# A two-layer hybrid decoder: who forms the low parts of the weights, and in what pieces

## The chip, the cores and the metric

The kernel runs on one core of a Trainium2 chip. The metric is the time of one execution on the device, in microseconds (us). The engines of a core go by short names here: PE is TensorE (matrix products; PEld is its loading of the stationary operand), DVE is VectorE, ACT is ScalarE, POOL is GpSimd, and SP is SyncE, which issues the transfers (DMA). Each engine works through its own queue in order.

## The reference

Two layers over 256 tokens of width 2048. Each layer is one mixer that adds to the residual stream; what matters here are its three products with large weights.

```python
for l in range(DEPTH):                      # DEPTH = 2
    shift, scale, gate = jnp.split(c_act @ w_ada[l] + b_ada[l], 3, axis=-1)
    h = rms_norm(x, norm_w[l]) * (1.0 + scale[:, None, :]) + shift[:, None, :]
    (gq, gk, gv, glr, gz, dq, dk, dv, da, db, dz, aq, ak, av, az) = jnp.split(h @ w_in[l], bounds, axis=-1)
    # o_gla: gated linear attention; o_gdn: gated delta rule; o_diff: differential softmax attention
    ...
    y = jnp.concatenate([o_gla, o_gdn, o_diff], axis=-1) @ w_out[l]
    x = x + gate[:, None, :] * y
```

All is float32: x is (1, 256, 2048), w_ada[l] 2048 x 6144, w_in[l] 2048 x 7704, w_out[l] 2048 x 2048.

## The kernel before

The program is written out in full (no loops on the device) and the order of each engine's instructions is chosen by a scheduler at build time, which goes by priorities: the weights' splitting and the modulation have priority AHEAD (1500), the mixers' steps 100000.

The modulation (w_ada) is one row vector times a matrix, so it is done on DVE: for each of the 24 groups of the two layers, eight transfers of 128 x 1024 land in a raw buffer, and DVE multiplies each by the vector and sums it along the row in one instruction (line 338, "rawa"). Layer 0's modulation and part of layer 1's run beside layer 0's input projection, and the rest beside what follows.

The input and output projections run on PE. To keep float32's precision with the faster float32r products, each factor is split into a high and a low part, and three products are summed: high by high, high by low, low by high. The activations' parts are hh and hl (lines 397 to 404; hn is the value before the split). The weights' parts are wh and wl. The function weights (line 303) does it: SP loads a chunk of up to 1024 columns into one of six raw buffers, which the modulation uses too (line 308, "raw"); the chunk is taken in pieces of at most 536 columns; ACT casts each piece to float32r (line 316, wh), and the difference to the raw piece is the low part (line 319, wl). A count decides the engine that subtracts: of each seven pieces in a row, three are given to POOL and four to DVE. There are five buffers each for wh and wl, of 536 columns.

project (line 433) uses a chunk in two ways. In the T form (tokens by columns) 512 columns of weights are the moving operand of two token tiles: six products per 512 columns, into the banks "pt". In the F form the weights are stationary, 128 columns at a time, into "pf". After the last k tile, or after each step's share of k tiles, the sums are added to what is there by DVE (line 450). out_project (line 1054) uses the weights as stationary operand, into "py", and DVE adds the gated sum to the residual (line 1200, xr). Between pieces poll() resumes the mixers, which are generators; they use all engines, and POOL does part of their elementwise work. Where the mixers take the mean square of heads, ACT writes the squares, which nobody reads, to a small tile, "junk".

Of the kernel before, what the change touches and what calls it, by code (L numbers as in the profile page):

```python
# [10 lines left out]
F32 = mybir.dt.float32  # L11
# [7 lines left out]
P = 128  # L19
D = 2048  # L20
KT = 16
T = 256
# [8 lines left out]
# The times (us) that the mixers' steps yield.  # L31
YW = {0: 7.0, 1: 8.0, 2: 25.0, 3: 1.25, 4: 2.0, 5: 2.0, 6: 15.0, 7: 2.5, 8: 11.25, 9: 3.25, 10: 6.0, 11: 4.0, 12: 2.94, 13: 0.75, 14: 1.5, 15: 3.0, 16: 3.0, 17: 3.5, 18: 2.0, 19: 3.75, 20: 6.25, 21: 7.5, 22: 3.75, 23: 10.0, 24: 14.0, 25: 0.75, 26: 3.75, 27: 7.0, 28: 2.25, 29: 12.0, 30: 4.2}

# Offsets of the input projection's columns, as the reference orders them.
# [19 lines left out]
# Blocks of columns in the order in which they are computed.  # L54
# [11 lines left out]
# The steps of each layer's input projection: blocks b0..b1-1 over k tiles k0..k1-1. (Layer 0's modulation arrives k tile  # L66
# by k tile, and layer 1's follows the norm.)
# [4 lines left out]
# The k tiles of the output projection's steps: gated linear attention, delta rule, differential attention.  # L72
# [3 lines left out]
def in_chunks(layer, i):  # L76
    """Chunks of w_in for one step: lists of (block, k0, k1) that share one transfer."""
# [23 lines left out]
def _chunk_pieces(chunk):  # L101
    """Sizes of the pieces, of whole k tiles, in which a chunk is split into two parts."""
    out = [0]
    for b, a, z in chunk:
        for _ in range(a, z):
            if out[-1] + _width(b) > 536:
                out.append(0)
            out[-1] += _width(b)
    return out


# Column layout of the packed per-partition parameters.
# [17 lines left out]
def _constants():  # L130
# [6 lines left out]
    # Of each chunk of 64 tokens, its own columns alone.  # L137
# [14 lines left out]
def hybrid_trunk(ctx: ExitStack, tc: tile.TileContext, x, cvec, pos, par, w_ada, w_in, w_out, w_lr, qkn, adt, cst, out):  # L152
# [7 lines left out]
    wsp = ctx.enter_context(tc.tile_pool(name="wsp", bufs=5))  # L160
# [8 lines left out]
    def reg(i, name):  # L169
        """One of the work tiles that the mixers hand on to each other, in the order of the program."""  # L170
        return work.tile([P, 512], F32, name=name, tag=f"R{i}", bufs=1)
# [4 lines left out]
    def bank(name, tag):  # L176
        """A PSUM bank. Each tag's banks are handed on in the order of the program: "a" delta rule and norm, "b" the other
        mixers, "p" projections."""
        return psum.tile([P, 512], F32, name=name, tag=tag, bufs=BANKS[tag])
# [4 lines left out]
    # The mixers are generators, resumed between pieces of the projections; they yield the tensor engine's time after which  # L184
    # their next step's inputs are expected, or a condition. PSUM banks and work tiles are handed on in this order.
# [46 lines left out]
    class Bank:  # L232
        """A PSUM bank (or half of its partitions) whose sums all rest on one clearing, by the first product. The products
        have to be issued in_order()."""
# [44 lines left out]
    junk = const.tile([P, 512], mybir.dt.bfloat16, name="junk")  # L279
# [21 lines left out]
    state = {"n": 0}  # L301

    def weights(src, sizes):
        """Loads sum(sizes) columns of weights and returns the two parts of each piece of them."""
        n = sum(sizes)
        raw = wraw.tile([P, RAW], F32, name="raw", tag="raw")
        with tc.high_priority(offset=AHEAD if state["n"] else 0):
            SP.dma_start(raw[:, 0:n], src)
        out, off = [], 0
        for m in sizes:  # L310
            r = raw[:, off:off + m]
            off += m
            wh = wsp.tile([P, 536], F32R, name="wh", tag="wh")[:, 0:m]
            wl = wsp.tile([P, 536], F32R, name="wl", tag="wl")[:, 0:m]
            with tc.high_priority(offset=AHEAD):
                ACT.copy(wh, r)  # L316
                state["n"] += 1
                e = POOL if state["n"] % POOL_WL[1] < POOL_WL[0] else DVE
                e.tensor_tensor(wl, r, wh.bitcast(F32), ALU.subtract)  # L319
            out.append((wh, wl))  # L320
        return out

# [1 line left out]
    ada = [const.tile([P, 3, KT], F32, name=f"ada{l}") for l in range(L)]  # L324

    def ada_group(l, g, raws=None):
        """Groups 0..7: scale and shift of k tiles 2g, 2g+1; groups 8..11: gate of k tiles 4(g-8)..+3."""
# [39 lines left out]
    def ada_mark(l, g):  # L367
        """Steps until the modulation's group g of layer l is done."""
        return 8 * (12 * l + g + 1)

# [4 lines left out]
    def rstd_rows(sqs):  # L375
        """sqs: tiles of squares whose sum over tiles and partitions is each token's. Returns its rstd on all partitions."""
# [20 lines left out]
    def modulate(l, xt, rb, hh, hl, k):  # L397
        """Two k tiles of the modulated input, in two parts."""
# [34 lines left out]
    def project(l, group, hh, hl, o, after):  # L433
# [18 lines left out]
        for chunk in in_chunks(l, group):  # L452
# [3 lines left out]
            parts = weights(src, _chunk_pieces(chunk))  # L456
            off = 0
            for b, a, z in chunk:
                kind = BLOCKS[b][0]
                w = _width(b)  # L460
                for k in range(a, z):
                    if off == parts[0][0].shape[1]:
                        parts.pop(0)
                        off = 0
                        poll()
                    wh, wl = parts[0]
# [624 lines left out]
    for l in range(L):  # L1091
# [132 lines left out]
        if l == 0:  # L1224
            sq = [temp("sqs", T, 1)]
# [81 lines left out]
```

## Time and profile before

| | |
|---|---|
| Median of 3 runs | 1144.73 us (1144.65 to 1145.38) |
| The profiled execution: span, first to last instruction | 1140.7 us |
| The profiled execution: whole time | not recorded apart; the median above lies 4.0 us over the span |
| PE busy | 1060.2 us (93%) |
| PEld busy | 927.9 us (81%) |
| DVE busy | 913.4 us (80%) |
| ACT busy | 613.7 us (54%) |
| POOL busy | 619.9 us (54%) |
| Read from memory | 267.76 MB, 238 GB/s over the span |

PE's products are pipelined and the ends of their records are modelled, so busy time of PE is not time at its peak. In stretches, the three projections and the mixers lie about so: layer 0's input projection from 27 to some 480 us, its output projection to 600 us, layer 1's input projection to some 1030 us, its output projection to the end.

### The profile page before, as it was taken

The numbers are of one execution on the slowest core, as the hardware profiler recorded it, in microseconds if no ns is written. First come the engines' busy times: TensorE is split into PE (matmuls) and PEld (weight loads), VectorE is DVE, ScalarE is ACT, GpSimd is POOL, SyncE is SP. The second block draws the span as 40 slices with busy tenths as digits, with TensorE's granted clock in tenths as the row PEclk, the third lists the DMA queues.
The fourth block names the chain that finished last, engine by engine and source line by source line (L and its number), as shares of the span: only waits on it lengthen the run. The fifth ranks groups of instructions, "written<-read, shape, count | busy, mean of one in ns | idle before, by whom it ended". The sixth has DMA issues, their size and how long they took to land.

```text
span 1140.7 us, 20595 instructions
## 1 busy us (share of the span) xinstructions
PE 1060.2 (93%) x7398; PEld 927.9 (81%) x7398; DVE 913.4 (80%) x1484; ACT 613.7 (54%) x1367; POOL 619.9 (54%) x550
## 2 busy tenths in 40 slices
PE   4989998889799999999988999998899999999998
PEld 3769876678788886898986877888799877879998
DVE  6899999998999759799788796767656877767853
ACT  4645434445654474666535545476454556557642
POOL 5444444456474586666753554366443666644642
PEclk9999999999999998999998999999899999999999
DMA  9888988888777454666689889785435555667462
GB/s 356 300 291 315 332 292 305 273 290 286 266 258 256 150 166 166 238 206 194 197 283 341 326 313 326 251 310 185 149 99 178 190 183 185 224 219 252 138 201 95
DMA packets 76807, 273.31 MB, mean 240 GB/s; under 512 B 8816, under 2 KB 9888, under 8 KB 76576
## 3 DMA queue, kind: packets, MB, share of 16 engines
q1 hardware_dynamic: 76704, 271.99, 69.8%
q8 instruction: 58, 0.95, 0.3%
q14 instruction: 45, 0.37, 0.1%
HBM read 267.76 MB, written 4.19 MB: 238 GB/s over the span
## 4 chain that ended last, share of the span: by engine, by line
PE 45%; DVE 25%; DMA 11%; issue 9%; POOL 5%; ACT 3%; SPq 0%; DVEq 0%; ACTq 0%; POOLq 0%
PE pt L191 21%; PE py L191 9%; DVE rawa L338 7%; DVE wl L319 7%; DMA rawa<-in_w_ada 7%; PE pf L191 6%; DMA raw<-in_w_in 4%; POOL wl L319 3%; DVE on_gdn L673 2%; PE Z_ps L191 1%; ACT wh L316 1%; PE o_gdn L191 1%; DVE z L450 1%; PE o_gla L191 1%; DVE hn L402 1%
## 5 line engine op out<-in xcount | busy, mean ns | idle before, releaser
L319 POOL TENSOR_TENSOR wl<-raw,wh 128x512 fp32r<-128x512 f32 (+2 forms) x266 | 403.8, 1532 | 355.8 <-ACT wh L316 319.1
L316 ACT CAST wh<-raw 128x512 fp32r<-128x512 f32 (+2 forms) x620 | 367.3, 613 | 311.2 <-PE pt L191 122.6
L338 DVE SCALAR_TENSOR_TENSOR rawa<-rawa,c_row 128x1024 f32<-128x1024 f32 x184 | 262.5, 1431 | 84.3 <-DMA rawa<-in_w_ada 73.0
L319 DVE TENSOR_TENSOR wl<-raw,wh 128x512 fp32r<-128x512 f32 (+2 forms) x354 | 285.5, 821 | 52.1 <-ACT wh L316 50.9
L191 PE MATMUL pt<-wl,hh 128*128 128x512 f32 (+1 forms) x768 | 294.1, 385 | 16.7 <-DVE wl L319 12.7
L191 PE MATMUL pt<-wh,hl 128*128 128x512 f32 (+1 forms) x768 | 289.2, 381 | 1.0 <-DVE hl L404 0.9
L191 PE MATMUL pt<-wh,hh 128*128 128x512 f32 (+1 forms) x768 | 257.4, 383 | 8.5 <-ACT hh L403 6.9
L191 PEld LDWEIGHTS pt<-wl,hh 128*128 128x128 f32 x768 | 146.3, 191 | 52.8 <-DVE wl L319 20.0
L191 PEld LDWEIGHTS pt<-wh,hh 128*128 128x128 f32 x768 | 144.5, 190 | 41.2 <-ACT hh L403 9.1
L191 PEld LDWEIGHTS pt<-wh,hl 128*128 128x128 f32 x768 | 145.8, 190 | 29.6 <-DVE hl L404 2.5
L191 PE MATMUL pf<-hh,wl 128*128 128x256 f32 x512 | 148.8, 292 | 6.4 <-POOL wl L319 4.0
L191 PE MATMUL pf<-hh,wh 128*128 128x256 f32 x512 | 148.2, 290 | 0.0
L191 PE MATMUL pf<-hl,wh 128*128 128x256 f32 x512 | 147.6, 289 | 0.0
L191 PEld LDWEIGHTS pf<-hh,wl 128*128 128x128 f32 x512 | 99.0, 194 | 9.5 <-POOL wl L319 4.9
L191 PEld LDWEIGHTS pf<-hh,wh 128*128 128x128 f32 x512 | 99.4, 194 | 2.3 <-issue 1.2
L191 PEld LDWEIGHTS pf<-hl,wh 128*128 128x128 f32 x512 | 99.1, 194 | 1.1 <-issue 0.7
L191 PE MATMUL py<-ogg,wh 128*128 128x256 f32 x512 | 99.4, 289 | 0.0
L191 PE MATMUL py<-odf,wh 128*128 128x256 f32 x512 | 91.6, 281 | 0.8 <-ACT odf L1044 0.7
L191 PEld LDWEIGHTS py<-ogg,wh 128*128 128x128 f32 x512 | 80.5, 189 | 0.9 <-issue 0.2
L191 PEld LDWEIGHTS py<-odf,wh 128*128 128x128 f32 x512 | 78.4, 188 | 1.5 <-ACT odf L1044 0.9
L191 PE MATMUL py<-odf,wl 128*128 128x256 f32 x256 | 72.0, 282 | 2.6 <-POOL wl L319 1.3
L191 PE MATMUL py<-ogg,wl 128*128 128x256 f32 x256 | 73.1, 287 | 0.0
(279 smaller groups left out, 1416.7 us busy)
## 6 DMA issues: line engine op xcount, KB each, us to landing
raw<-in_w_in SPq DMA_DIRECT2D x224, 512.0 KB, 4.6
rawa<-in_w_ada SPq DMA_DIRECT2D x184, 512.0 KB, 4.7
raw<-in_w_out SPq DMA_DIRECT2D x64, 512.0 KB, 4.2
raw<-in_w_in SPq DMA_DIRECT2D x20, 402.0 KB, 4.1
fr<-in_w_ada SPq DMA_DIRECT2D x8, 512.0 KB, 9.9
xt<-in_x SPq DMA_DIRECT2D x4, 512.0 KB, 5.3
xr<-in_x SPq DMA_DIRECT2D x4, 512.0 KB, 7.8
xs<-xr SPq DMA_DIRECT2D x1, 2048.0 KB, 11.7
```

The source lines that it names most:

```text
L191: return PE.matmul(o, lhsT=lhsT, rhs=rhs, start=start, stop=stop, **kw)
L316: ACT.copy(wh, r)
L319: e.tensor_tensor(wl, r, wh.bitcast(F32), ALU.subtract)
L338: DVE.scalar_tensor_tensor(raw, raw, 1.0, cb, ALU.mult, ALU.mult, accum_out=sums[:, i:i + 1])
L402: DVE.scalar_tensor_tensor(h, rb, scale, xt[:, i, :], ALU.mult, ALU.mult)
L450: DVE.tensor_tensor(d, src, d, ALU.add)
L673: DVE.scalar_tensor_tensor(yi[:, s:T], src[:, 0:T - s], pcol("conv", w + 3 - s), yi[:, s:T], ALU.mult, ALU.add)
```

## The change

weights takes a chunk whole: one cast of up to 1024 columns on ACT, one subtraction of the same width on DVE. POOL forms no low parts any more, and the count that chose the engine is gone. The buffers for wh and wl are three each, of 1024 columns. project asks poll() at the same places as before, and out_project takes its slices from the one chunk. To make room, the tile for the squares of heads has 256 columns in place of 512, and the sum of squares at the end of layer 0 lies in a work tile. Comments and docstrings are taken out, so that the line numbers of the changed kernel are lower.

```diff
-    wsp = ctx.enter_context(tc.tile_pool(name="wsp", bufs=5))
+    wsp = ctx.enter_context(tc.tile_pool(name="wsp", bufs=3))
...
-    junk = const.tile([P, 512], mybir.dt.bfloat16, name="junk")
+    junk = const.tile([P, 256], mybir.dt.bfloat16, name="junk")
...
-    def weights(src, sizes):
-        n = sum(sizes)
-        raw = wraw.tile([P, RAW], F32, name="raw", tag="raw")
+    def weights(src, n):
+        raw = wraw.tile([P, RAW], F32, name="raw", tag="raw")[:, 0:n]
+        wh = wsp.tile([P, RAW], F32R, name="wh", tag="wh")[:, 0:n]
+        wl = wsp.tile([P, RAW], F32R, name="wl", tag="wl")[:, 0:n]
         with tc.high_priority(offset=AHEAD if state["n"] else 0):
-            SP.dma_start(raw[:, 0:n], src)
-        out, off = [], 0
-        for m in sizes:
-            r = raw[:, off:off + m]
-            off += m
-            wh = wsp.tile([P, 536], F32R, name="wh", tag="wh")[:, 0:m]
-            wl = wsp.tile([P, 536], F32R, name="wl", tag="wl")[:, 0:m]
-            with tc.high_priority(offset=AHEAD):
-                ACT.copy(wh, r)
-                state["n"] += 1
-                e = POOL if state["n"] % POOL_WL[1] < POOL_WL[0] else DVE
-                e.tensor_tensor(wl, r, wh.bitcast(F32), ALU.subtract)
-            out.append((wh, wl))
-        return out
+            SP.dma_start(raw, src)
+        with tc.high_priority(offset=AHEAD):
+            ACT.copy(wh, raw)
+            DVE.tensor_tensor(wl, raw, wh.bitcast(F32), ALU.subtract)
+        state["n"] += 1
+        return wh, wl
...
-            parts = weights(src, _chunk_pieces(chunk))
-            off = 0
+            wh, wl = weights(src, n)
+            off, polled = 0, 0
...
-                    if off == parts[0][0].shape[1]:
-                        parts.pop(0)
-                        off = 0
+                    if off + w - polled > 536:
+                        polled = off
                         poll()
-                    wh, wl = parts[0]
...
-            a = junk_n[0] % (512 // width) * width
+            a = junk_n[0] % (256 // width) * width
...
-            parts = weights(src, [512, 512])
+            wh, wl = weights(src, 1024)
...
-                wh, wl = parts[i // 4]
-                s = slice(128 * (i % 4), 128 * (i % 4) + 128)
+                s = slice(128 * i, 128 * i + 128)
...
-            sq = [temp("sqs", T, 1)]
+            sq = [reg(9, "sqs")[:, 0:T]]
...
-POOL_WL = (3, 7)
```

Two places show what the scheduler made of it. A row is a line number, an operation, what it writes and reads, its size, and how many follow each other alike. The first is DVE at the start of layer 0's input projection, before the change; fr and rawa are the modulation's products, hn and hl the split of the modulated input.

```order
L402 SCALAR_TENSOR_TENSOR hn<-rb,ada_144,xt 128x256 x2
L404 SCALAR_TENSOR_TENSOR hl<-hn,ada_144,hh 128x256
L319 TENSOR_TENSOR wl<-raw,wh 128x512
L404 SCALAR_TENSOR_TENSOR hl<-hn,ada_144,hh 128x256
L338 SCALAR_TENSOR_TENSOR rawa,ada_p<-rawa,c_row 128x1024
L319 TENSOR_TENSOR wl<-raw,wh 128x512 x2
L338 SCALAR_TENSOR_TENSOR rawa,ada_p<-rawa,c_row 128x1024
```

The same place of the changed kernel.

```order
L384 SCALAR_TENSOR_TENSOR hn<-rb,ada_144,xt 128x256 x2
L301 TENSOR_TENSOR wl<-raw,wh 128x1024
L386 SCALAR_TENSOR_TENSOR hl<-hn,ada_144,hh 128x256
L301 TENSOR_TENSOR wl<-raw,wh 128x1024
L320 SCALAR_TENSOR_TENSOR rawa,ada_p<-rawa,c_row 128x1024
L386 SCALAR_TENSOR_TENSOR hl<-hn,ada_144,hh 128x256
L301 TENSOR_TENSOR wl<-raw,wh 128x1024
L320 SCALAR_TENSOR_TENSOR rawa,ada_p<-rawa,c_row 128x1024
```

A chunk's subtraction now stands between two products of the modulation where one or two pieces stood, and the first one stands ahead of hl. The second place is POOL in the middle of layer 0's delta rule, before the change; C, on_gdn, fm and E are the mixer's.

```order
L761 TENSOR_TENSOR E<-E,ct 128x512
L319 TENSOR_TENSOR wl<-raw,wh 128x512 x3
L799 TENSOR_TENSOR C<-Lm,ct 128x512
L319 TENSOR_TENSOR wl<-raw,wh 128x512 x2
L799 TENSOR_TENSOR C<-Lm,ct 128x512
L319 TENSOR_TENSOR wl<-raw,wh 128x512
L828 TENSOR_TENSOR on_gdn<-fm 128x512
```

The same place of the changed kernel.

```order
L741 TENSOR_TENSOR E<-E,ct 128x512
L779 TENSOR_TENSOR C<-Lm,ct 128x512
L808 TENSOR_TENSOR on_gdn<-fm 128x512
L919 TENSOR_TENSOR scr<-aqk,rtab 128x4x64 x2
L808 TENSOR_TENSOR on_gdn<-fm 128x512
```

POOL's queue holds the mixers' work alone.

## Rows read from the trace of the kernel before

**Rows 1.** The page's span, and busy us, share and instructions of each engine.

```profile
span 1140.7 us, 20595 instructions
PE 1060.2 (93%) x7398; PEld 927.9 (81%) x7398; DVE 913.4 (80%) x1484; ACT 613.7 (54%) x1367; POOL 619.9 (54%) x550
```

**Rows 2.** Stretches: busy us of PE, PEld, DVE, ACT, POOL; clock, DMA share, GB/s.

```profile
27.00:360.00 333.00, 304.47 (x1822) 258.57 (x1824) 317.16 (x492) 170.05 (x329) 166.47 (x124) 0.98 0.84 289
360.00:600.00 240.00, 227.04 (x1871) 203.59 (x1866) 198.41 (x354) 135.12 (x357) 156.25 (x152) 0.97 0.61 204
600.00:760.00 160.00, 153.44 (x778) 127.38 (x779) 123.94 (x196) 84.94 (x164) 76.67 (x53) 0.97 0.88 314
760.00:1141.00 381.00, 364.44 (x2893) 328.66 (x2891) 257.10 (x415) 212.73 (x501) 206.21 (x208) 0.99 0.55 179
```

**Rows 3.** PE's waits, 27 to 360 us: us in total, times, longest.

```profile
PE pt L191 <- DVE wl L319: 8.3, 7, 2.4
...
PE pt L191 <- POOL wl L319: 2.9, 4, 1.2
PE pf L191 <- DVE wl L319: 2.3, 3, 0.9
...
PE pf L191 <- POOL wl L319: 1.6, 2, 1.4
```

**Rows 4.** PE's waits, 360 to 1141 us.

```profile
PE pt L191 <- DVE wl L319: 4.4, 6, 2.4
...
PE pf L191 <- POOL wl L319: 2.4, 1, 2.4
...
PE py L191 <- POOL wl L319: 1.3, 2, 0.8
```

**Rows 5.** Instructions of DVE, 27 to 360 us: count, busy us, mean ns, idle before.

```profile
L338 DVE SCALAR_TENSOR_TENSOR rawa<-rawa,c_row 128x1024 f32<-128x1024 f32 x86 | 125.7, 1465 | 1.5 <-DMA rawa<-in_w_ada 1.3 <-issue 0.2
L319 DVE TENSOR_TENSOR wl<-raw,wh 128x512 fp32r<-128x512 f32 x102 | 86.8, 869 | 9.4 <-ACT wh L316 9.4
L450 DVE TENSOR_TENSOR z<-pt,z 128x512 f32<-128x512 f32 x24 | 16.1, 678 | 0.0
...
L402 DVE SCALAR_TENSOR_TENSOR hn<-rb,ada,xt 128x256 f32<-128x256 f32 x14 | 11.2, 843 | 0.1
L404 DVE SCALAR_TENSOR_TENSOR hl<-hn,ada,hh 128x256 fp32r<-128x256 f32 x16 | 10.1, 651 | 0.6 <-ACT hh L403 0.6
```

**Rows 6.** Single instructions of DVE while POOL was idle: start us, us.

```profile
604.88 1.22 DVE L338 SCALAR_TENSOR_TENSOR rawa<-rawa,c_row 128x1024 f32<-128x1024 f32 x1
...
607.97 0.48 DVE L404 SCALAR_TENSOR_TENSOR hl<-hn,ada,hh 128x256 fp32r<-128x256 f32 x1
...
1091.15 0.68 DVE L319 TENSOR_TENSOR wl<-raw,wh 128x512 fp32r<-128x512 f32 x1
```

**Rows 7.** Instructions of POOL, in order of time: start us, us.

```profile
600.95 1.26 POOL L319 TENSOR_TENSOR wl<-raw,wh 128x512 fp32r<-128x512 f32 x1
...
1095.39 4.09 POOL L319 TENSOR_TENSOR wl<-raw,wh 128x512 fp32r<-128x512 f32 x3 [6.50 <-ACT wh L316]
```

**Rows 8.** Instructions of POOL, 27 to 360 us, the costliest group.

```profile
L319 POOL TENSOR_TENSOR wl<-raw,wh 128x512 fp32r<-128x512 f32 x77 | 124.6, 1635 | 137.2 <-ACT wh L316 128.7 <-DVE rawa L338 8.3 <-POOL wl L319 0.2
```

**Rows 9.** Stretches of 40 us.

```profile
80.00:120.00 40.00, 39.20 (x282) 36.30 (x281) 39.54 (x62) 23.29 (x54) 17.30 (x13) 1.00 0.88 313
120.00:160.00 40.00, 38.42 (x165) 30.55 (x164) 39.90 (x57) 17.39 (x30) 19.29 (x12) 1.00 0.88 306
...
640.00:680.00 40.00, 39.66 (x170) 31.39 (x170) 33.71 (x48) 22.08 (x41) 19.31 (x12) 1.00 0.85 304
```

**Rows 10.** Instructions of ACT, whole span: the casts, and the squares of x.

```profile
L316 ACT CAST wh<-raw 128x512 fp32r<-128x512 f32 (+2 forms) x620 | 367.3, 613 | 311.2 <-PE pt L191 122.6 <-DMA raw<-in_w_in 69.2 <-PE py L191 42.7
...
L1082 ACT ACTIVATE sqx<-xt 128x1024 f32<-128x1024 f32 x4 | 4.2, 1057 | 1.8 <-DMA xt<-in_x 1.7
```

**Rows 11.** Waits of all engines, whole span: us in total, times, longest.

```profile
ACT wh L316 <- PE pt L191: 122.6, 142, 3.5
DVE rawa L338 <- DMA rawa<-in_w_ada: 73.0, 44, 4.6
```

More of the change, by code (lines that the diff above doesn't have):

```diff
@@ L98, in _chunk_elems @@
     return sum((z - a) * _width(b) for b, a, z in chunk)
[L101 to L108, printed above, removed]
-    return out
 PAR = {}
@@ L301, in hybrid_trunk @@
     state = {"n": 0}
-    def weights(src, sizes):
-        n = sum(sizes)
-        raw = wraw.tile([P, RAW], F32, name="raw", tag="raw")
+    def weights(src, n):
+        raw = wraw.tile([P, RAW], F32, name="raw", tag="raw")[:, 0:n]
+        wh = wsp.tile([P, RAW], F32R, name="wh", tag="wh")[:, 0:n]
+        wl = wsp.tile([P, RAW], F32R, name="wl", tag="wl")[:, 0:n]
         with tc.high_priority(offset=AHEAD if state["n"] else 0):
-            SP.dma_start(raw[:, 0:n], src)
-        out, off = [], 0
-        for m in sizes:
-            r = raw[:, off:off + m]
-            off += m
-            wh = wsp.tile([P, 536], F32R, name="wh", tag="wh")[:, 0:m]
-            wl = wsp.tile([P, 536], F32R, name="wl", tag="wl")[:, 0:m]
-            with tc.high_priority(offset=AHEAD):
-                ACT.copy(wh, r)
-                state["n"] += 1
-                e = POOL if state["n"] % POOL_WL[1] < POOL_WL[0] else DVE
-                e.tensor_tensor(wl, r, wh.bitcast(F32), ALU.subtract)
-            out.append((wh, wl))
-        return out
+            SP.dma_start(raw, src)
[4 more added lines that the diff above has]
+        return wh, wl
     ada = [const.tile([P, 3, KT], F32, name=f"ada{l}") for l in range(L)]
```

## The prediction, made before the changed kernel ran

> **What bounds the kernel now.** I read the page's first part before anything else: a span of 1140.7 us, TensorE (PE) busy for 93% of it, VectorE (DVE) for 80%, GpSimd (POOL) and ScalarE (ACT) for 54% each [rows 1]. Those shares are means over stages with different limits, so the second view is the table of stretches [rows 2]. It shows two kinds of stage. From 27 to 360 us (layer 0's input projection, with the modulation's products running beside it) DVE is busy for 317.2 of 333 us and PE is idle for 333 - 304.5 = 28.5 us: DVE is the limit. From 360 us on DVE is busy for 198.4 + 123.9 + 257.1 = 579.4 of 781 us and PE is idle for 781 - (227.0 + 153.4 + 364.4) = 36 us: PE is mostly the limit. The third view, what PE waited for, agrees: in the first stretch the low parts of the weights, wl, are what ends PE's named waits, 8.3 + 2.3 us when DVE formed them and 2.9 + 1.6 us when POOL did [rows 3]. After 360 us no such group is over 4.4 us, and the two that end with POOL's wl have 2.4 and 1.3 us [rows 4].
>
> The fourth view is the list of DVE's instructions in the first stretch [rows 5], read against single ones at a moment when POOL does nothing [rows 6]. The reader is to see that the same instruction has two prices. A product of the modulation (rawa, 1024 columns, two inputs from SBUF) takes 1.22 us alone and 1.465 us on the mean; a low part of 512 columns takes 0.68 alone and 0.869 on the mean; but the sum into z of 512 columns, one of whose inputs is in PSUM, takes 0.678 us on the mean of 24, which is what it would take alone. So something that hits only instructions with two SBUF inputs stretches them. POOL's own low part takes 1.26 us in a quiet moment [rows 7] and 1.635 on the mean [rows 8], so it is stretched too.
>
> The Trainium skill has this as a rule ("SBUF — State Buffer", Who interferes with whom): a VectorE instruction with two SBUF inputs and a GpSimd instruction that reads SBUF take one read port in turn, each for its whole length. The trace agrees as to which instructions suffer (0.678 against 0.869 us); what the rule would give in full is the third rival.
>
> **The change, part by part.**
>
> Removed from POOL: all its subtractions. In the first stretch these are 77 of 512 columns, 124.6 us [rows 8] of the 166.5 us that POOL is busy there [rows 2]. What is left on POOL is the mixers' work.
>
> Gained on DVE in the first stretch, if the stretching goes: rawa 86 x (1.465 - 1.21) = 21.9 us; low parts 102 x (0.869 - 0.68) = 19.3; hn, of hl's width, 14 x (0.843 - 0.48) = 5.1; hl 16 x (0.651 - 0.48) = 2.7 [rows 5, 6]. Together 49.0 us. Part of this is the doing of POOL's other instructions, which stay; smaller groups that I don't count gain as well. I let these two cancel.
>
> Added on DVE: 102 + 77 = 179 pieces of 512 become 89.5 chunks. No 1024-column subtraction is in the trace; the nearest row is rawa, which has the same width and also two SBUF inputs: 1.22 us. The lower bound is 0.68 us (no dearer than one piece), the upper 2 x 0.68 = 1.36. I take 1.21. So 89.5 x 1.21 = 108.3 us in place of 102 x 0.68 = 69.4 (their price without the stretching): +38.9. The few pieces of 536 and 268 columns are left out on both sides. Sum for DVE in the stretch: 38.9 - 49.0 = -10.1 us. Its ends: if the stretching is not POOL's doing, +38.9; if everything else there gains as well, the stretch can give at most PE's idle time, -28.5. In 80 of the 333 us PE is already busy for 39.2 and 38.4 of 40 [rows 9], where a faster DVE buys little; against this stand the small groups left out. I take -10.
>
> After 360 us DVE gets more work and loses stretching in the same way, and it has 201.6 us of idle time to hide what is left over. What goes there are PE's waits for POOL's low parts, 2.4 + 1.3 us [rows 4]. Which pieces went to POOL was counted out as three in a row of seven, so three stand in a queue: 4.09 us for three [rows 7], while PE uses up three pieces of its wide kind in 3 x 6 x 0.235 = 4.2 us (170 matmuls in 40 us [rows 9]). I take -4.
>
> ACT: 620 casts [rows 10] become one per chunk, about half as many. The nearest row for 1024 columns is the square of x, 1.06 us [rows 10], below 2 x 0.62, so ACT's total falls. It was busy for 54%, so at nothing; if the cast were on the path, one chunk costs 0.44 us more latency than one piece.
>
> Buffers: five pieces of 536 columns become three chunks of 1024. ACT is often held until PE gives a buffer back (122.6 us in 142 waits [rows 11]), so the parts run as far ahead as the buffers allow. When PE leaves a buffer now, four pieces are ahead of it, 4 x 6 x 0.235 = 5.6 us, and the refill takes 0.62 + 0.87: 4.1 us are left for queues. Then two chunks are ahead, 5.6 us again, and the refill takes 1.06 + 1.21: 3.3 us are left. I cost this at nothing as long as DVE's queue is shorter than that; the slower rival is the case where it is not.
>
> The page "Perfetto Trace Analysis" of the Trainium skill speaks against this part (Optimizing Scalar/DVE Operations): where those engines are not saturated but cause bubbles elsewhere, smaller instructions let work finish sooner. Here that is the stretch after 360 us, and by it the 0.8 us of lost margin would show as new waits of PE for wl; the trace of before cannot show that.
>
> DMA: the same transfers in the same order. A raw buffer is given back by one engine rather than two. The first stretch moves 289 GB/s with the DMA engines busy for 0.84; 10 us less makes that 0.87, and 640 to 680 us shows 0.85 with PE at 39.7 of 40 [rows 2, 9], so nothing is late there next. The smaller scratch tile for the squares of heads and the other place of one sum are on ACT and POOL and not on a path: nothing.
>
> Sum: -10 - 4 = -14 us. The profiled execution spans 1140.7 us, 4.0 us less than the median of the runs, 1144.73; the same 4 us stand around the new span: 1126.7 + 4.0 = 1131 us.
>
> **Rivals.**
>
> 1. No change (1142 to 1147). DVE's saving is taken in wherever PE is full already, and the end is set by PE from 360 us on. For it: PE is at 99% from 640 to 680 us [rows 9]. Against it: the 28.5 us of PE's idle time stand in the very stretch in which DVE is full.
>
> 2. Slower, by DVE's queue (1148 to 1162, say 1154). DVE works in order; where a product of the modulation waits for its transfer (73.0 us in 44 waits, up to 4.6 us [rows 11]), every low part behind it stands still. Now three pieces of seven pass by on POOL; after it none do. It decides when a wait plus the product itself, 1.21 us, is over the 3.3 us of margin: a wait of 4.6 is over by 2.5. If 10 of the 44 waits are so placed: 25 us; less the 14 gained, +11, and with fewer of them some +5. Against it: PE needs the pieces in order, so a piece that passes by helps only as far as the next one on DVE.
>
> 3. Much faster (1105 to 1117). If each of POOL's subtractions shut DVE out for its whole 1.26 us, 77 of them cost it 97 us, against 38.9 added: 58 us of DVE time, cut by PE's idle 28.5 us to a gain of 28.5 + 4, 1112 us. That is the port rule taken in full. Against it: the rows show 49.0 us lost to 77 subtractions, 0.64 us each, since POOL stands aside for the other half.
>
> **How the numbers follow.** My forecast, 1118 to 1141 us, has a chance of 0.54; the much faster case 0.11; no change 0.10; slower by DVE's queue 0.25. What can be told from no change is 0.2%, 2.3 us. So faster 0.54 + 0.11 = 0.65, same 0.10, slower 0.25. The range takes in most of the much faster case and the lower half of the slower one: 1109 to 1153 us. The likeliest case's own range is 1118 to 1141.
>
> **What would show it.** Right: rawa's mean in the first stretch falls from 1.465 to about 1.25 us, the 1024-column subtraction takes 1.2 to 1.3, DVE's busy time before 360 us shrinks although it does all low parts, layer 0's input projection ends some 10 us sooner, and no wait of PE ends with POOL's wl. Wrong: rawa stays near 1.46 (then the stretching isn't POOL's and the time goes up by tens of us); the chunk subtraction is far over 1.3; or PE's waits for DVE's wl after 360 us, 4.4 us now [rows 4], grow to 15 or more, which is the second rival.

## The result, and the profile after

The changed kernel takes 1130.31 us (median of 4 runs, 1128.9 to 1133.62), against 1145.06 us for the kernel before in the same runs: 0.986 of it, interval 0.9835 to 0.9885. The forecast was 1131. The sum was right, but its terms were not: two were too small, and a loss between them had no term at all, as the stages below show.

The first part of the page answers to [rows 1]: POOL's busy time falls from 619.9 to 228.3 us, and DVE, which now does all low parts, has 12 us less to do and not more.

```profile
span 1128.0 us, 19525 instructions
PE 1056.3 (94%) x7398; PEld 922.2 (82%) x7398; DVE 901.6 (80%) x1442; ACT 575.0 (51%) x1060; POOL 228.3 (20%) x284
```

The stretches, with the columns of [rows 2]. The first ends 13 us earlier on the clock and holds the same 86 products rawa; in it DVE has 296.4 us of work in place of 317.2. The ends of the next two lie 10 us earlier but not at the same work (up to 750 us PE has done 89 products fewer than up to 760 us before), so the marks further below decide there.

```profile
27.00:347.00 320.00, 300.17 (x1778) 256.48 (x1780) 296.44 (x477) 158.24 (x229) 30.28 (x37) 0.99 0.87 304
347.00:590.00 243.00, 227.40 (x1880) 200.41 (x1876) 194.53 (x333) 124.80 (x299) 85.45 (x104) 0.96 0.57 190
590.00:750.00 160.00, 148.52 (x724) 122.03 (x725) 121.58 (x190) 75.88 (x106) 1.04 (x1) 0.97 0.87 309
750.00:1128.00 378.00, 369.38 (x2980) 333.56 (x2978) 272.61 (x416) 205.66 (x413) 98.08 (x128) 1.00 0.57 188
```

DVE's instructions from 27 to 347 us answer to [rows 5]. The mean of rawa falls from 1465 to 1237 ns and hl's from 651 to 479; z, with an input in PSUM, had 678 and has 681. The new subtraction has 1189 on the mean, narrower chunks included; the first line is the group of before that it answers to, with its narrower pieces.

```profile
L319 DVE TENSOR_TENSOR wl<-raw,wh 128x512 fp32r<-128x512 f32 (+2 forms) x115 | 95.5, 847 | 10.7 <-ACT wh L316 10.7
...
L301 DVE TENSOR_TENSOR wl<-raw,wh 128x1024 fp32r<-128x1024 f32 (+1 forms) x103 | 122.0, 1189 | 11.5 <-ACT wh L300 11.2
L320 DVE SCALAR_TENSOR_TENSOR rawa<-rawa,c_row 128x1024 f32<-128x1024 f32 x86 | 106.0, 1237 | 11.4 <-DMA rawa<-in_w_ada 11.3
L432 DVE TENSOR_TENSOR z<-pt,z 128x512 f32<-128x512 f32 x24 | 15.7, 681 | 0.0
...
L653 DVE SCALAR_TENSOR_TENSOR on_gdn<-fm,pt,on_gdn 128x255 f32<-128x255 f32 (+2 forms) x21 | 10.8, 522 | 0.0
...
L386 DVE SCALAR_TENSOR_TENSOR hl<-hn,ada,hh 128x256 fp32r<-128x256 f32 x16 | 7.5, 479 | 0.2 <-ACT hh L385 0.2
...
L384 DVE SCALAR_TENSOR_TENSOR hn<-rb,ada,xt 128x256 f32<-128x256 f32 x15 | 6.6, 477 | 0.0
```

PE's waits from 347 us on answer to [rows 4]. None can end with POOL's wl any more; those that end with DVE's have 6.3 + 1.6 + 1.0 us.

```profile
PE pt L180 <- DVE wl L301: 6.3, 7, 3.2
...
PE py L180 <- DVE wl L301: 1.6, 3, 0.7
...
PE pf L180 <- DVE wl L301: 1.0, 1, 1.0
```

**Stage by stage.** To see where the 13 us of span came from, one needs the same piece of work in both traces. The last "pt" product of layer 0's input projection is one such mark (PE's products into a tile: count, shortest/median/longest ns, first and last start). Before, in a window from 440 us:

```profile
L191 PE MATMUL pt<-wh,hl x24: 389/394/628, 440.0 to 471.8; 128*128 128x512 f32 x24
```

And after: 453.8 in place of 471.8, so the projection ends 18.0 us sooner.

```profile
L180 PE MATMUL pt<-wh,hl x13: 392/394/502, 440.2 to 453.8; 128*128 128x512 f32 x13
```

POOL's first instruction of layer 1's norm (rs) marks the end of layer 0. Before, then after (start us, us, instruction, idle before it):

```profile
599.71 1.14 POOL L373 TENSOR_TENSOR rs<-ms,mhalf 128x2 f32<-128x2 f32 x1 [6.41 <-ACT ms L389]
```

```profile
598.97 1.04 POOL L355 TENSOR_TENSOR rs<-ms,mhalf 128x2 f32<-128x2 f32 x1 [12.61 <-ACT ms L371]
```

Of the 18.0 us only 0.7 are left. From this mark to the span's end it is 541.0 us before and 529.0 after: 12.0 us come from layer 1. So the total is 0.7 + 12.0, and layer 0 gave back 17.3 us between 454 and 599.

Where it gave them back is in PE's products of the mixers, layer 0, in the order of the chain: the delta rule's doubling steps (Z_ps), its output (o_gdn), the scores of the attention (s_ps), its output (o_diff), and the out-projection's last k tiles, which need it (py<-odf). Before:

```profile
L191 PE MATMUL Z_ps<-Y,Tm x160: 218/218/267, 358.9 to 400.9; 64*64 64x64 f32 x160
L191 PE MATMUL o_gdn<-S_gdn,fm x24: 272/273/474, 449.3 to 478.1; 128*64 128x128 f32 x24
L191 PE MATMUL s_ps<-aqk x48: 271/275/377, 478.3 to 512.9; 128*128 128x128 f32 x48
L191 PE MATMUL o_diff<-av,scr x24: 377/378/382, 499.6 to 540.4; 128*128 128x256 f32 x24
L191 PE MATMUL py<-odf,wh x256: 274/280/387, 543.4 to 594.4; 128*128 128x256 f32 x128
```

After:

```profile
L180 PE MATMUL Z_ps<-Y,Tm x160: 218/218/267, 368.8 to 429.4; 64*64 64x64 f32 x160
L180 PE MATMUL o_gdn<-S_gdn,fm x24: 272/273/473, 461.3 to 484.4; 128*64 128x128 f32 x24
L180 PE MATMUL s_ps<-aqk x48: 270/275/377, 484.6 to 515.5; 128*128 128x128 f32 x48
L180 PE MATMUL o_diff<-av,scr x24: 377/380/636, 510.6 to 540.9; 128*128 128x256 f32 x24
L180 PE MATMUL py<-odf,wh x256: 276/279/493, 539.4 to 592.6; 128*128 128x256 f32 x128
```

The first doubling step comes 10 us later than before and the last 28 us later. The scores start 0.2 us after the last o_gdn in both kernels, and the last o_diff stands at 540.4 and 540.9. The projection hurries ahead; the chain behind the delta rule does not. POOL's queue shows what may be a part of it: after, a step's C stands behind the power (r_d) and the rope products (scr) of the queries' and keys' norm, which the earlier projection has made ready at the same time. How much this costs the chain isn't shown.

```profile
380.90 2.49 POOL L355 TENSOR_TENSOR r_d<-r_d,mhalf 128x8 f32<-128x8 f32 x1
383.36 2.00 POOL L779 TENSOR_TENSOR C<-Lm,ct 128x512 f32<-128x512 f32 x1
...
388.82 2.49 POOL L919 TENSOR_TENSOR scr<-aqk,rtab 128x256 f32<-128x256 f32 x2
...
402.10 1.26 POOL L779 TENSOR_TENSOR C<-Lm,ct 128x512 f32<-128x512 f32 x1
```

In layer 1 the gain is in the stretch in which its mixers begin. Before (columns of [rows 2]), with two pieces of it:

```profile
740.00:880.00 140.00, 128.58 (x1399) 121.08 (x1399) 90.98 (x140) 77.97 (x172) 75.70 (x75) 0.96 0.56 185
...
770.00:780.00 10.00, 7.63 (x52) 7.43 (x51) 9.64 (x15) 7.98 (x16) 6.63 (x7) 0.83 0.51 160
...
810.00:820.00 10.00, 7.51 (x65) 6.50 (x64) 7.25 (x10) 1.24 (x2) 3.53 (x3) 0.82 0.47 165
```

After:

```profile
740.00:870.00 130.00, 124.07 (x1410) 117.27 (x1409) 89.31 (x135) 73.86 (x141) 38.48 (x48) 1.00 0.61 200
```

About the same 1400 products take 10 us less. PE's idle time falls from 11.4 to 5.9 us, and its busy time by 4.5, as the granted clock goes from 0.96 to 1.00: before, PE idled for 2.4 and 2.5 us in the two pieces of 10 us, and the clock averaged 0.83 and 0.82 there, part of the time at the lower of its two levels, 1.2 GHz.

### The profile page after: what moved, and what is told of

Read it like the earlier page. It is cut to its first block, busy times and chain, and to the rows that moved or that the text cites. A ratio compares the mean times of both kernels' runs of the same rounds, so it can differ in the third digit from the quotient of the medians.

```text
span 1128.0 us, 19525 instructions
## 1 busy us (share of the span) xinstructions
PE 1056.3 (94%) x7398; PEld 922.2 (82%) x7398; DVE 901.6 (80%) x1442; ACT 575.0 (51%) x1060; POOL 228.3 (20%) x284
## 4 chain that ended last, share of the span: by engine, by line
PE 35%; DMA 7%; DVE 5%; issue 4%; ACT 1%; POOL 0%; SPq 0%; DVEq 0%; ACTq 0%; POOLq 0%
PE pt L180 16%; PE py L180 8%; DMA rawa<-in_w_ada 6%; PE pf L180 5%; DVE wl L301 3%; DVE rawa L320 1%; PE Z_ps L180 1%; DMA xr<-xs 1%; PE o_gdn L180 1%; PE Y_ps L180 0%; PE s_ps L180 0%; PE ropeT_ps L184 0%; PE oT_ps L184 0%; PE o_diff L180 0%; PE S_ps L180 0%
## 5 line engine op out<-in xcount | busy, mean ns | idle before, releaser
L300 ACT CAST wh<-raw 128x1024 fp32r<-128x1024 f32 (+1 forms) x312 | 320.2, 1029 | 351.8 <-PE pt L180 184.6
L301 DVE TENSOR_TENSOR wl<-raw,wh 128x1024 fp32r<-128x1024 f32 (+1 forms) x312 | 382.7, 1232 | 67.0 <-ACT wh L300 66.5
L320 DVE SCALAR_TENSOR_TENSOR rawa<-rawa,c_row 128x1024 f32<-128x1024 f32 x184 | 230.5, 1258 | 83.3 <-DMA rawa<-in_w_ada 82.8
L180 PE MATMUL pt<-wh,hh 128*128 128x512 f32 (+1 forms) x768 | 275.5, 386 | 15.9 <-ACT hh L385 11.2
L180 PE MATMUL pf<-hh,wh 128*128 128x256 f32 x512 | 143.9, 282 | 3.5 <-ACT wh L300 3.1
L180 PE MATMUL pf<-hh,wl 128*128 128x256 f32 x512 | 142.7, 283 | 2.8 <-DVE wl L301 2.7
L180 PE MATMUL pf<-hl,wh 128*128 128x256 f32 x512 | 143.9, 282 | 0.0
L180 PEld LDWEIGHTS pf<-hh,wh 128*128 128x128 f32 x512 | 96.1, 188 | 5.3 <-ACT wh L300 3.6
L180 PEld LDWEIGHTS pf<-hh,wl 128*128 128x128 f32 x512 | 95.1, 188 | 4.8 <-DVE wl L301 3.7
L1179 DVE SCALAR_TENSOR_TENSOR xr<-py,ada,xr 128x256 f32<-128x256 f32 x96 | 45.5, 476 | 24.1 <-PE py L180 20.8
## 6 DMA issues: line engine op xcount, KB each, us to landing
fr<-in_w_ada SPq DMA_DIRECT2D x8, 512.0 KB, 10.3
```

Source lines behind the costliest of these rows:

```text
L180: return PE.matmul(o, lhsT=lhsT, rhs=rhs, start=start, stop=stop, **kw)
L300: ACT.copy(wh, raw)
L301: DVE.tensor_tensor(wl, raw, wh.bitcast(F32), ALU.subtract)
L320: DVE.scalar_tensor_tensor(raw, raw, 1.0, cb, ALU.mult, ALU.mult, accum_out=sums[:, i:i + 1])
L1179: DVE.scalar_tensor_tensor(xr[:, c, :], d, ada[l][:, 2, c:c + 1], xr[:, c, :], ALU.mult, ALU.add)
```

## The experiments

Each was timed against the kernel before on the same chip, and the ratio is to that kernel. It took 1148.6 to 1150.2 us there (medians), against 1145.06 beside the changed kernel, so runs of different experiments are compared by their ratios; the changed kernel's is 0.986. The first four ask where the gain comes from, the next four why layer 0 kept nothing, the last four what the size of the pieces is worth.

**1. The kernel before, with no subtraction on POOL.**

```diff
-POOL_WL = (3, 7)
+POOL_WL = (0, 7)
```

> The kernel before with one number changed: no piece of 512 or 536 columns goes to POOL, all low parts are formed by DVE; five buffers of 536 columns stay. Theory A (the gain is the end of POOL's reads from SBUF beside DVE's two-input instructions): rawa's mean falls from 1.43 to about 1.25 us as in the changed kernel, but DVE pays 0.68 us for each of 620 pieces, some 40 us more busy time than with chunks; most of the gain, 1133 to 1139 us. Theory B (the gain is the halved number of casts and subtractions): no gain, 1145 to 1165 us. Theory C (the gain is that POOL's own queue is free for the mixers and that no low part comes late in threes): 1131 to 1136 us whatever DVE's busy time.

1123.67 us, 0.9777 (0.9751 to 0.9804). The pieces, the five buffers and everything else are those of before. DVE's two costliest groups:

```profile
L319 DVE TENSOR_TENSOR wl<-raw,wh 128x512 fp32r<-128x512 f32 (+2 forms) x620 | 425.9, 705 | 63.5 <-ACT wh L316 61.8
L338 DVE SCALAR_TENSOR_TENSOR rawa<-rawa,c_row 128x1024 f32<-128x1024 f32 x184 | 226.3, 1232 | 68.8 <-DMA rawa<-in_w_ada 68.4
```

That is below the range of every theory. Taking POOL out gives the whole gain, and some more; joining the pieces into chunks gives none. The wide subtraction does save DVE time, 382.7 us for 312 against 425.9 for 620, but the span doesn't get shorter by it (9 asks for this alone). What this run can't tell is whether POOL's reads cost the time or POOL's full queue; 3 and 4 part the two.

**2. The changed kernel, three chunks of seven on POOL.**

```diff
-            DVE.tensor_tensor(wl, raw, wh.bitcast(F32), ALU.subtract)
-        state["n"] += 1
+            state["n"] += 1
+            e = POOL if state["n"] % 7 < 3 else DVE
+            e.tensor_tensor(wl, raw, wh.bitcast(F32), ALU.subtract)
```

> The changed kernel, but of each seven chunks three have their low part formed by POOL, 1024 columns in one instruction (about 2.5 us). Theory A: rawa back at 1.4 us or more and no gain, 1143 to 1160 us. Theory B: the gain stays, 1130 to 1137 us. Theory C: POOL's queue is as full as before and each of its low parts is 1 us later than two pieces were, 1148 us or more.

1175.04 us, 1.0224 (1.0193 to 1.0254).

```profile
L303 POOL TENSOR_TENSOR wl<-raw,wh 128x1024 fp32r<-128x1024 f32 (+2 forms) x134 | 355.9, 2663 | 346.5 <-ACT wh L300 316.8
...
L321 DVE SCALAR_TENSOR_TENSOR rawa<-rawa,c_row 128x1024 f32<-128x1024 f32 x184 | 308.7, 1688 | 91.1 <-DMA rawa<-in_w_ada 90.3
```

With POOL back, rawa is stretched to 1688 ns, more than before the change. PE's waits that end with wl come back too, 10.3 us for POOL's and 15.7 for DVE's into pt. The time is over theory A's range and fits C, but here POOL both reads and delivers late, so the run doesn't part the two either.

**3 and 4. The changed kernel, with POOL reading SBUF to no purpose, and with POOL only writing.** After six of seven wide subtractions POOL works in place on the raw buffer, which nobody needs any more; in 4 it only fills it.

```diff
+            if n == RAW and state["n"] % 7 < 6:
+                POOL.tensor_tensor(raw[:, 0:512], raw[:, 0:512], raw[:, 512:1024], ALU.subtract)
...
+            if n == RAW and state["n"] % 7 < 6:
+                POOL.memset(raw, 0.0)
```

> The changed kernel, and after each subtraction, for six chunks of seven, POOL subtracts one half of the used raw buffer from the other half, in place: 512 columns, two inputs from SBUF, as many instructions of that kind as POOL had before. The result is used by nobody; DVE does all low parts. Theory A: rawa's mean goes back to about 1.4 us and the chunk's subtraction to about 1.4, DVE gets some 60 us more to do, 1145 to 1165 us. Theory B: no change against the changed kernel, 1129 to 1134 us. Theory C: the mixers queue behind POOL again, but no low part does, 1133 to 1142 us with rawa at 1.25.

> As the run with POOL's extra subtractions, at the same places and as often, but POOL fills the used raw buffer with zeros (1024 columns, about 1.05 us, no input from SBUF). It holds POOL's queue and the raw buffer for about as long. Theory A: rawa stays at 1.25 us and the time at 1129 to 1135 us, since POOL reads nothing. Theory B: the same, 1129 to 1134. Theory C: as slow as the run with the extra subtractions, 1133 to 1142.

Reading: 1240.29 us, 1.0799 (1.0771 to 1.0827). Writing: 1143.24 us, 0.9951 (0.993 to 0.9972). The groups of the reading kernel:

```profile
L303 POOL TENSOR_TENSOR raw<-raw 128x512 f32<-128x512 f32 x247 | 419.7, 1704 | 474.6 <-DVE wl L301 356.8
...
L301 DVE TENSOR_TENSOR wl<-raw,wh 128x1024 fp32r<-128x1024 f32 (+1 forms) x312 | 426.3, 1373 | 48.7 <-ACT wh L300 48.5
L322 DVE SCALAR_TENSOR_TENSOR rawa<-rawa,c_row 128x1024 f32<-128x1024 f32 x184 | 258.4, 1409 | 68.6 <-DMA rawa<-in_w_ada 60.2
...
L434 DVE TENSOR_TENSOR z<-pt,z 128x512 f32<-128x512 f32 x40 | 26.0, 678 | 0.0
```

And of the writing one:

```profile
L303 POOL MEMSET raw<- 128x1024 f32 x247 | 235.5, 955 | 555.0 <-DVE wl L301 428.9
L301 DVE TENSOR_TENSOR wl<-raw,wh 128x1024 fp32r<-128x1024 f32 (+1 forms) x312 | 382.9, 1232 | 70.0 <-ACT wh L300 69.6
L322 DVE SCALAR_TENSOR_TENSOR rawa<-rawa,c_row 128x1024 f32<-128x1024 f32 x184 | 228.6, 1244 | 93.8 <-DMA rawa<-in_w_ada 91.3
```

The same 247 places in POOL's queue: the reads stretch rawa to 1409 ns and wl to 1373, the writes leave both alone, and z, with its PSUM input, stays at 678 even beside the reads. That is the mechanism. With the writes, layer 0's input projection still ends where it does in the changed kernel (its last pt at 454.9 us, against 453.8; with the reads at 505.1):

```profile
L180 PE MATMUL pt<-wh,hl x80: 390/394/496, 361.4 to 454.9; 128*128 128x512 f32 x80
```

So what POOL's instructions take there is taken by their reads and not by the time that POOL is busy. Both times miss the ranges on record. The price of the reads is larger than was expected: DVE is busy for 1052.8 us in place of 901.6, 0.61 us for each read, and most of these 151 us find no cover. The writes are not free either: the run is over theory C's range too, layer 0 ends at 609.1 us in place of 599.0, while the rest takes 530.6 against 529.0. That cost falls between the projection's end and layer 0's, where the mixers' steps stand in POOL's queue. A write holds POOL and the raw buffer but leaves DVE's instructions at their price, so the cost belongs to queues and buffers; the two were not separated.

**5 and 6. The delta rule cut short in layer 0, in the changed kernel and in the kernel before.** The same edit in both leaves out three of the five doubling steps, so that the output is no longer the reference's:

```diff
-        for n in range(1, 6):
+        for n in (range(1, 6) if l else (3, 5)):
```

> The changed kernel with three of the five doubling steps of the delta rule's inversion left out in layer 0 (about 8 us of PE's work and 45 us of that chain's length in the changed kernel, 30 us in the kernel before). Theory F (in the changed kernel the end of layer 0 is set by that chain and the attention behind it, which is why the 17 us that layer 0's input projection gained are gone by its end): layer 0's last output projection ends 15 us or more sooner and the whole at 1108 to 1118 us. Rival G (the end of layer 0 is set by PE's and DVE's total work): 8 us less, 1120 to 1125.

> The kernel before with the same three doubling steps left out in layer 0. Theory F: there the input projection's own pace sets more of layer 0's end, so the cut gains less than it does in the changed kernel: 1134 to 1142 us, and the distance between the two kernels grows from 15 to 20 us or more. Rival G: the same 8 us as in the changed kernel, 1135 to 1139, and the distance stays at 15.

In the changed kernel: 1109.88 us, 0.9653 (0.9622 to 0.9685), about 2% under the changed kernel. In the kernel before: 1151.56 us, 1.0022 (1.0 to 1.0044), nothing, a miss: both theories had it faster, at 1134 to 1142. The chain in the changed kernel with the short delta rule:

```profile
L180 PE MATMUL o_gdn<-S_gdn,fm x24: 272/273/323, 428.6 to 452.1; 128*64 128x128 f32 x24
...
L180 PE MATMUL s_ps<-aqk x48: 270/275/275, 468.8 to 490.9; 128*128 128x128 f32 x48
L180 PE MATMUL o_diff<-av,scr x24: 378/379/635, 496.9 to 522.3; 128*128 128x256 f32 x24
```

The last o_diff moves from 540.9 to 522.3, and the end of layer 0 from 599.0 to 581.2. So the gain of the input projection was there to be had, and the delta rule's chain held it back. PE's shorter work alone doesn't explain it: the cut takes 13.4 us of its busy time away (1056.3 to 1042.9), less than layer 0's end moves, and in the kernel before the same cut moves that end from 599.7 to 596.7 only. There the projection's pace seems to set it: with the short chain the scores start 18.6 us after the projection's last pt (468.3 to 486.9), much as in the changed kernel with the cut (22.9 us, 445.9 to 468.8). In the kernel before with the cut, layer 1 got longer in the profiled run, though the edit is not in it:

```profile
737.00:867.00 130.00, 117.70 (x1164) 111.09 (x1162) 80.87 (x123) 72.14 (x161) 67.66 (x71) 0.93 0.55 177
```

The clock is 0.93 in that stretch, where 740 to 880 us had 0.96 before. Runs of the kernel before lay between 1142.7 and 1153.6 us on that chip, so a run of it may have more or less of such a stretch; what sets how much is open.

**7 and 8. The kernel of experiment 1, the delta rule's steps first; and its C on DVE as well.** In 7 the scheduler ranks the delta rule's steps above all other mixers; 8 adds the second edit.

```diff
-URG = {"gdn": 100000, "gla": 100000, "qk": 100000, "att": 100000, "gate": 100000}
+URG = {"gdn": 200000, "gla": 100000, "qk": 100000, "att": 100000, "gate": 100000}
...
-            (DVE if n == 1 else POOL).tensor_tensor(all8(C), all8(Lm), m64("lev", 64 * n), ALU.mult)
+            DVE.tensor_tensor(all8(C), all8(Lm), m64("lev", 64 * n), ALU.mult)
```

> The kernel with pieces and no POOL, and the delta rule's steps at twice the priority of the other mixers'. If layer 0's end hangs on the delta rule because the other mixers take DVE and POOL from it, its doubling steps come closer together and the time falls by some 3 to 8 us, 1115 to 1121. Rival (the priority hardly changes the order): 1122 to 1126.

> As the run with pieces, no POOL and the delta rule first, and the masked product C of each doubling step is formed by DVE (0.68 us) in place of POOL (1.3 to 2 us and POOL's queue). If POOL's queue is what spreads the doubling steps: 3 to 8 us less than that run. Rival (DVE's queue is as long): no change, or 1 to 3 us more.

7: 1131.06 us, 0.9833 (0.9815 to 0.9852), slower than without the rank (0.9777), a miss: the doubling steps did end sooner (last Z_ps at 422.4 in place of 435.6), but o_gdn's last product moved to 491.7 from 490.5. 8: 1122.27 us, 0.9755 (0.9735 to 0.9775), 9 us better than 7. The delta rule's output in 7, then in 8:

```profile
L191 PE MATMUL o_gdn<-S_gdn,fm x24: 272/273/324, 468.3 to 491.7; 128*64 128x128 f32 x24
```

```profile
L191 PE MATMUL o_gdn<-S_gdn,fm x24: 272/273/324, 460.9 to 482.2; 128*64 128x128 f32 x24
```

9.5 us sooner, and layer 0 ends 9.0 us sooner (599.0 to 590.0). It isn't the doubling steps that gain them: the last Z_ps stands at 428.5, later than in 7. What lies between that and o_gdn was not taken apart. With 1 it is the best version here, by the ratios about 1% under the changed kernel; the two can't be told apart.

The end of layer 0 follows the chain in the kernels of this table, which have the whole delta rule. Starts in us, from the rows of the tiles, in one profiled execution of each:

| kernel | projection's last pt | last o_gdn | first s_ps | last o_diff | layer 1's norm | from there to the end |
|---|---|---|---|---|---|---|
| before | 471.8 | 478.1 | 478.3 | 540.4 | 599.7 | 541.0 |
| after | 453.8 | 484.4 | 484.6 | 540.9 | 599.0 | 529.0 |
| 1 (pieces, no POOL) | 446.1 | 490.5 | 490.7 | 537.5 | 595.4 | 526.1 |
| 4 (POOL writes) | 454.9 | 500.2 | 500.4 | 545.2 | 609.1 | 530.6 |
| 7 (delta rule first) | 441.4 | 491.7 | 491.9 | 540.4 | 599.0 | 529.0 |
| 8 (and C on DVE) | 437.8 | 482.2 | 482.5 | 532.3 | 590.0 | 528.5 |
| 9 (half subtractions) | 449.1 | 499.6 | 499.8 | 545.9 | 605.3 | 526.7 |
| 11 (halves of both) | 447.0 | 501.3 | 501.7 | 550.6 | 611.4 | 531.4 |

Three things stand out. An early projection alone doesn't end layer 0 early: 11 has its last pt 6.8 us before the changed kernel's and its norm 12.4 us after. The norm comes 58 to 64 us after the last o_diff, whatever came ahead. And the last column falls from 541.0 to between 526 and 532 in every kernel here without POOL's subtractions, in 4 too, where POOL is busy with writes; 6 and 12, which keep the subtractions, have 555.8 and 548.3. So layer 1 gains some 10 us or more in each, while layer 0's end lies anywhere from 590 to 611 us.

**9. The changed kernel, the chunk's subtraction in two halves.**

```diff
-            DVE.tensor_tensor(wl, raw, wh.bitcast(F32), ALU.subtract)
+            for i in range(0, n, 536 if n % 512 else 512):
+                j = min(n, i + (536 if n % 512 else 512))
+                DVE.tensor_tensor(wl[:, i:j], raw[:, i:j], wh[:, i:j].bitcast(F32), ALU.subtract)
```

> The changed kernel, one cast per chunk and three buffers of 1024 columns as there, but the low part is formed by two subtractions of half the chunk, both on DVE. The run with pieces and no POOL was 6 us faster than the changed kernel although DVE does more. Theory D (the whole-chunk subtraction costs, because the low part comes in one late lump): the time comes down to that run's, 1121 to 1127 us. Rival (the subtraction's size costs nothing, the 6 us come from the cast's size, from the buffers or from the order): 1129 to 1138 us, DVE being busier by some 35 us.

1134.33 us, 0.9869 (0.9836 to 0.9901): as the changed kernel, though DVE is busy for 928.0 us in place of 901.6. The size of the subtraction is worth nothing that can be told.

**10. The changed kernel with two buffers.**

```diff
-    wsp = ctx.enter_context(tc.tile_pool(name="wsp", bufs=3))
+    wsp = ctx.enter_context(tc.tile_pool(name="wsp", bufs=2))
```

> The changed kernel with two buffers of 1024 columns for each part in place of three. Theory (the prediction's margin: with three, a buffer's refill of 1.06 + 1.21 us has 5.6 us of PE's work ahead of it; with two it has 2.8 us, 0.5 us of margin): PE waits for the weights at many chunks, 1160 to 1220 us. Rival (three are more than enough, the buffers never set the pace): 1128 to 1136 us.

1193.77 us, 1.038 (1.0346 to 1.0414). PE's waits, the whole span:

```profile
PE pt L180 <- DVE wl L301: 46.6, 56, 3.7
PE pf L180 <- DVE wl L301: 16.1, 12, 2.8
```

With one chunk less ahead, PE waits 68 times for a low part into these two, 62.7 us in all, where the changed kernel has 9.3 (6.6 + 2.7); the span grows by 62.8 (1128.0 to 1190.8). The third buffer is what makes the wide chunk bearable.

**11. The changed kernel with halves of both, cast and subtraction, in three buffers of 1024.** The loop of 9, with the cast in it.

```diff
+                ACT.copy(wh[:, i:j], raw[:, i:j])
```

> The changed kernel with both instructions in halves (two casts and two subtractions per chunk), in the same three buffers of 1024 columns; no POOL. Left open between the changed kernel and the run with pieces and no POOL (7 us faster): the size of the cast, or the buffers (five of 536 against three of 1024). If the cast's size costs: 1121 to 1127 us. If the buffers or the order that the scheduler makes of them: 1130 to 1138.

1144.5 us, 0.996 (0.9936 to 0.9984), a miss for every theory. ACT and DVE work on the pieces of experiment 1, and by the ratios it is almost 2% slower than that. The pieces' size is therefore not what makes 1 faster than the changed kernel. The two differ in the buffers, in the small tiles (12) and in the order that the scheduler makes; in the profiled executions 16 of 21 us are in layer 0 (its norm at 611.4 against 595.4). Which of them it is stays open. Against 9 only the casts are halved as well, and it costs about 1%; why is open too.

**12. The kernel before with the small tiles.** junk with 256 columns, the sum of squares in a work tile.

```diff
-    junk = const.tile([P, 512], mybir.dt.bfloat16, name="junk")
+    junk = const.tile([P, 256], mybir.dt.bfloat16, name="junk")
...
-            sq = [temp("sqs", T, 1)]
+            sq = [reg(9, "sqs")[:, 0:T]]
```

> The kernel before with only the small parts of the change: the tile for the squares of heads at 256 columns, and layer 0's sum of squares in a work tile. The prediction costs these at nothing: 1142 to 1148 us. Rival (ACT waits for itself twice as often at the smaller tile, on the mixers' chains): 1149 us or more.

1151.58 us, 1.0011 (0.9987 to 1.0035): nothing. That the time lies in the rival's range is the chip's doing: the kernel before took 1150.2 us beside it.

## Why the prediction was right, and where it was not

**The mechanism: right, and shown for the first stretch and for layer 1.** POOL's reads of SBUF stretched DVE's instructions with two SBUF inputs. Experiment 1 takes the reads away and has the gain, 3 puts reads back and loses it many times over, 4 puts only writes there: the stretching stays out, and the projection and layer 1 keep their gain. What 4 does lose, it loses in layer 0's mixers, which the prediction did not look at. The signs that were named came: rawa at 1237 ns (1250 forecast), the wide subtraction at 1.22 us alone (1.21 taken) as here at a moment when POOL is idle,

```profile
609.65 1.23 DVE L301 TENSOR_TENSOR wl<-raw,wh 128x1024 fp32r<-128x1024 f32 x1 [0.78 <-ACT wh L300]
612.45 1.22 DVE L301 TENSOR_TENSOR wl<-raw,wh 128x1024 fp32r<-128x1024 f32 x1 [1.57 <-ACT wh L300]
```

and no wait of PE for POOL's wl. This last sign could not fail, since POOL forms none.

**"I take -10" in the first stretch: too small.** DVE's work there fell by 317.2 - 296.4 = 20.8 us, and the projection ended 18.0 us sooner. The groups that the sum counts gave almost nothing: rawa -19.7, hn -4.6, hl -2.6, but the low parts, all widths, +26.5 (95.5 to 122.0) where the sum has +19.6. The other 20 us came from groups that it left out; the 21 sums into on_gdn went from 14.8 to 10.8 us, the ten small sums into ada_s from 6.2 to 2.0. So the step at fault is "I let these two cancel": POOL's other instructions kept little of the stretching, and the small groups gained in full.

**The step that failed: that what the first stretch gains reaches the end.** Its loss was put at nothing, without a reason; the first rival comes nearest, but has PE's fullness take the saving in. From 360 us on the prediction asked only what PE waits for, and [rows 4] showed no wait for the delta rule, since PE was fed by a projection that was late itself. It did not ask what has to follow the projection in any case. That is the chain delta rule, attention, last k tiles of the out-projection; it ran as late as before, and took back 17.3 of 18.0 us. Experiments 5 and 6 show it: the same cut of the chain is worth 18 us of layer 0 in the changed kernel and 3 in the one before. Why the doubling steps themselves run later than before stays open.

**"-4" after 360 us: mis-sized, and for layer 1 by a factor of three.** 2.4 + 1.3 us of waits for POOL's wl were counted. The 12.0 us of layer 1 hold 5.5 us of PE's idle time in the stretch from 740 us, several mixers' waits among them, and 4.5 us of PE's own time that went with the higher granted clock. So here the pauses and the lower clock together cost about twice the pauses' length, as read from one profiled execution of each kernel. That the misses cancelled (+17 against -8 and -8) is luck.

**The rivals.** No change: out. DVE's queue, with 15 us or more of waits for wl: out, these came to 8.9 us after 347 us, a little more than before. But its margin is real, as two buffers show. Much faster, by the port in full: out as to size. Each of the 247 reads of experiment 3 cost DVE 0.61 us, close to the 0.64 that the prediction read from the rows, and far from POOL's whole instruction, 1.26 us in a quiet moment [rows 7]. The Trainium skill's rule on who interferes with whom ("SBUF — State Buffer") names the right instructions, and the traces agree with it in that. That DVE loses POOL's whole instruction each time is the rival's reading of it, and that is what the 0.61 us rule out. "POOL stands aside for the other half" is more than the rows show: POOL's own subtraction grew by 0.375 us, from 1.26 to 1.635.

**The costs taken as nothing.** The small tiles: right (12). The cast and the subtraction of twice the width: right as to size, 1029 ns for the cast where 1.06 us was taken, and halves of the subtraction gain nothing (9). The advice of the Trainium skill for smaller instructions ("Perfetto Trace Analysis", Optimizing Scalar/DVE Operations) finds no support in 9 (0.9869) or 11 (0.996). The transfers: right, the DMA engines' share of the first stretch is 0.87, as worked out. The buffers, three of 1024 for five of 536: not settled. By the ratios the changed kernel is about 1% behind the same work in pieces (0.986 against 0.9777), and the pieces in its buffers another 1% behind that (11, 0.996). An edit here also changes the scheduler's order, and the end of layer 0 lies anywhere from 590 to 611 us in the table, so that no run gives the buffers' own price.

## What to carry to other kernels

Work that is given to GpSimd is not free for VectorE: if it reads SBUF, price it by what it adds to each VectorE instruction with two SBUF inputs, and look whether VectorE alone would be done sooner. Before a gain in a stage is put into the sum, follow the longest chain that must come after that stage's work; where that chain doesn't move, the gain stays in the middle. Where a scheduler re-orders the program, compare stage by stage between marks that both traces have, since a right total can hide wrong terms.

## What the runs showed of the hardware that was not expected

POOL's fill of 128 x 1024 takes 955 ns and leaves VectorE's two-input instructions at their price (1232 and 1244 ns), while its subtraction of half that width stretches them to 1373 and 1409 and is itself stretched from 1.26 to 1.70 us. On POOL the wide subtraction, 2663 ns on the mean beside DVE's work, took a little more than two narrow ones in a quiet moment (2 x 1.26 us), and stretched rawa more (1688 ns) than 512 columns at a time did (1431 on the mean of the whole span).
